# A short convolution's projections by Strassen's scheme, and a first stage with three modulators on TensorE

## The chip, the cores and the metric

The kernel runs on one core of one Trainium2 chip. The metric is the device time of one execution in microseconds, as the median of the runs shown. Engines are named TensorE (PE in the rows, PEld for its weight loads), VectorE (DVE), ScalarE (ACT), GpSimd (POOL) and SyncE (SP, which issues most DMAs).

## The reference

Two blocks work on 512 tokens of width 1024, all in fp32. The first is an adaptively normalised attention block. Its modulators are products of one vector `c` with a 1024 x 3072 matrix; the first third shifts and the second scales the normalised input:

```
mod = c @ w_ada[l] + b_ada[l]
shift, scale, gate = jnp.split(mod, 3, axis=-1)
h = rms_norm(x, g_pre[l]) * (1.0 + scale[:, None, :]) + shift[:, None, :]
proj = h @ w_in[l]
```

Attention of several kinds and two output projections follow. The second block puts 16 meta tokens ahead (528 tokens) and runs a gated short convolution and then an mLSTM mixer. The convolution, where most of the change lies, is

```
proj = u @ w_in                                   # (528 x 1024) @ (1024 x 8192)
b_gate, c_gate, xin, z = jnp.split(proj, 4, axis=-1)
y = conv_general_dilated(c_gate * xin, w_conv, ...)  # width 3, per channel
return (jax.nn.silu(z) * b_gate * y) @ w_out      # (528 x 2048) @ (2048 x 1024)
```

## The kernel before

Every fp32 operand of a large product is split in two fp32r parts, high and low, and each product is three matmuls (high by high, high by low, low by high; `mm3`). Activations lie with channels on the partitions: `uh` and `ul` hold the parts of the block's input as 8 slices of 128 channels by 528 tokens. A weight unit is a tile of 128 x 1024 that SP loads into a ring of three (`wst`); ScalarE writes its high part (`whi`), VectorE the low part (`wlo`), each a ring of three. The class `Weights` hands the units out in the order of a list.

The instructions are not issued in the order of the source. `Plan` notes each operation with its reads and writes, and at the end of each phase a list scheduler (`flush`) fills one queue per engine from modelled durations (`cost`) and priorities (the order of the source, plus `plan.prio`). On the chip each queue then runs in order and waits on semaphores.

First stage: the input `x1` comes in eight DMAs; ScalarE squares it, TensorE sums the columns and spreads the reciprocal root (`stat_cols`, `cols_bc`). For each of 8 slices k a megabyte of `w_ada` is loaded (`ada`, a ring of three), VectorE multiplies it by `c` and sums it (`ada_mac`, 9 instructions on 128 x 256), TensorE turns the sum into two columns (`modmm`), ScalarE makes the high part of h and a copy (`mkh`), VectorE the low part, and 18 matmuls of 512 columns take it in. GpSimd normalises slices 2 to 7 and makes the weights' low parts. Runs of matmuls of ones (`warm`) lie between.

Convolution: 16 steps f, each with four units (c, x, z, b) of 128 output channels. A unit's 528 tokens are two halves of 264 columns with a PSUM bank each: 2 halves x 8 slices x 3 = 48 matmuls. VectorE takes the banks out: c times `rb2`, times x, the three-tap convolution, z times `rb` and through tanh, b; GpSimd does two of the multiplications. After steps 4, 8, 12 and 15 `conv_out` projects four steps' results back (192 matmuls, four weight units) and adds them to `x1`.

## Time and profile before

| | us |
|---|---|
| median of 3 runs (lowest, highest) | 1488.86 (1488.4, 1491.43) |
| the profiled execution | 1492.32 |
| its span, first to last instruction | 1490.3 |
| TensorE busy in the span | 1453.2 |
| VectorE busy | 881.8 |
| ScalarE, GpSimd busy | 605.7, 251.5 |

The mean granted TensorE clock was 0.986 of full speed. A busy TensorE is not one at its peak: matmuls overlap, and the time from one start to the next is what counts. The same holds on VectorE, whose rows overlap by some 0.08 us.

### The profile page before, as it was taken

How to read it: one execution, taken by the hardware profiler on the slowest of the kernel's cores; microseconds unless marked ns; L12 is line 12 of the kernel's file. 1: busy time of each engine (PE TensorE's matmuls, PEld its weight loads, DVE VectorE, ACT ScalarE, POOL GpSimd, SP SyncE). 2: the span in 40 equal slices, each digit the busy share in tenths (PEclk: the TensorE clock that was granted, in tenths of full speed). 3: DMA queues.
4: the chain of work that ended last, by engine and by line, in shares of the span. 5: the costliest groups of instructions: out<-in, count | busy, mean ns of one | idle time of the engine just before them, and what ended most of it. 6: DMA issues, size and time to landing. Idle time of an engine off the chain costs nothing.

```text
span 1490.3 us, 22552 instructions
## 1 busy us (share of the span) xinstructions
PE 1453.2 (98%) x8965; PEld 1296.9 (87%) x8965; DVE 881.8 (59%) x1710; ACT 605.7 (41%) x1103; POOL 251.5 (17%) x296
## 2 busy tenths in 40 slices
PE   6899999999998999999999999999999999999997
PEld 5687888878898999999999999978878888887886
DVE  6976868786858745545445445755434635443465
ACT  3465747775256322122122122554333433433333
POOL 3220313342003111011010011302002001100201
PEclk7999999999998999999999999999999999999999
DMA  6535121013553222232222222321222222132221
GB/s 219 191 127 164 58 81 47 29 44 125 210 163 113 86 100 85 86 100 86 97 88 86 99 86 79 100 71 57 99 85 71 85 85 85 57 100 85 72 71 57
DMA packets 44120, 142.60 MB, mean 96 GB/s; under 512 B 5744, under 2 KB 12144, under 8 KB 42608
## 3 DMA queue, kind: packets, MB, share of 16 engines
q1 hardware_dynamic: 43440, 136.98, 27.7%
q0 software_dynamic: 576, 4.19, 0.8%
q8 instruction: 70, 1.15, 0.3%
q14 instruction: 34, 0.28, 0.1%
HBM read 139.06 MB, written 2.10 MB: 95 GB/s over the span
## 4 chain that ended last, share of the span: by engine, by line
PE 91%; DVE 6%; ACT 1%; DMA 1%; issue 0%; POOL 0%; SPq 0%; DVEq 0%; POOLq 0%; ACTq 0%
PE bank L255 91%; DVE mac L255 2%; DVE wlo L255 1%; DMA x<-in_xT 0%; DVE zt L255 0%; DVE ul L255 0%; DMA wst<-in_wm 0%; DVE P L255 0%; POOL P L255 0%; ACT whi L255 0%; ACT P L255 0%; DVE pl L255 0%; SPq L255 0%; DVE ak L255 0%; DVE so L255 0%
## 5 line engine op out<-in xcount | busy, mean ns | idle before, releaser
L255 PE MATMUL bank<-uh,whi 128*128 128x264 f32 (+1 forms) x1784 | 574.2, 326 | 3.2 <-ACT uh L255 2.1
L255 PE MATMUL bank<-ul,whi 128*128 128x264 f32 (+1 forms) x1784 | 572.2, 325 | 0.0
L255 PE MATMUL bank<-uh,wlo 128*128 128x264 f32 (+1 forms) x1768 | 568.4, 325 | 1.8 <-DVE wlo L255 1.8
L255 ACT CAST whi<-wst 128x1024 fp32r<-128x1024 f32 (+2 forms) x236 | 244.7, 1038 | 606.0 <-PE bank L255 445.6
L255 DVE TENSOR_TENSOR wlo<-wst,whi 128x1024 fp32r<-128x1024 f32 (+1 forms) x227 | 280.3, 1236 | 177.5 <-ACT whi L255 176.3
L255 PEld LDWEIGHTS bank<-uh,whi 128*128 128x128 f32 x1784 | 337.0, 189 | 28.9 <-ACT uh L255 3.7
L255 PEld LDWEIGHTS bank<-ul,whi 128*128 128x128 f32 x1784 | 336.7, 189 | 24.5 <-DVE ul L255 0.2
L255 PEld LDWEIGHTS bank<-uh,wlo 128*128 128x128 f32 x1768 | 334.3, 189 | 26.3 <-DVE wlo L255 2.2
L255 DVE TENSOR_TENSOR zr<-bank,rb 128x264 f32<-128x264 f32 (+1 forms) x64 | 35.8, 560 | 120.8 <-PE bank L255 120.8
L255 DVE TENSOR_TENSOR x<-x,bank 128x264 f32<-128x264 f32 (+2 forms) x102 | 49.8, 496 | 69.5 <-PE bank L255 67.4
L255 POOL TENSOR_TENSOR yv<-yv,rb 128x528 f32<-128x528 f32 x16 | 21.2, 1324 | 332.1 <-DVE yv L255 332.1
L255 PE MATMUL bank<-gh,wlo 128*128 128x264 f32 x256 | 72.5, 284 | 0.0
L255 PE MATMUL bank<-gl,whi 128*128 128x264 f32 x256 | 72.4, 283 | 0.0
L255 PE MATMUL bank<-gh,whi 128*128 128x264 f32 x256 | 72.3, 284 | 0.0
L255 POOL TENSOR_SCALAR P<-P,sm 128x256 f32<-128x256 f32 (+3 forms) x96 | 52.2, 562 | 81.9 <-DVE sm L255 41.4
L255 PE MATMUL bank<-whi,uh 128*128 128x512 f32 (+1 forms) x160 | 61.7, 386 | 0.3 <-DVE ak L255 0.3
L255 PE MATMUL bank<-wlo,uh 128*128 128x512 f32 (+1 forms) x160 | 61.7, 386 | 0.0
L255 PE MATMUL bank<-whi,ul 128*128 128x512 f32 (+1 forms) x160 | 61.6, 385 | 0.0
L255 ACT ACTIVATE P<-P,nm 128x256 f32<-128x256 f32 (+3 forms) x96 | 50.9, 531 | 9.8 <-DVE nm L255 8.6
L255 PE MATMUL bank<-Gh,whi 128*128 128x512 f32 (+1 forms) x144 | 53.5, 371 | 0.0
L255 PE MATMUL bank<-Gl,whi 128*128 128x512 f32 (+1 forms) x144 | 53.3, 370 | 0.0
L255 PE MATMUL bank<-Gh,wlo 128*128 128x512 f32 (+1 forms) x144 | 53.3, 370 | 0.0
(338 smaller groups left out, 2283.1 us busy)
## 6 DMA issues: line engine op xcount, KB each, us to landing
wst<-in_wci SPq DMA_DIRECT2D x64, 512.0 KB, 3.4
wst<-in_wqkv SPq DMA_DIRECT2D x32, 512.0 KB, 3.4
wst<-in_wzo SPq DMA_DIRECT2D x32, 512.0 KB, 3.4
wst<-in_wm SPq DMA_DIRECT2D x23, 512.0 KB, 3.5
wst<-in_wout SPq DMA_DIRECT2D x16, 512.0 KB, 4.0
wst<-in_wco SPq DMA_DIRECT2D x16, 512.0 KB, 3.4
wst<-in_wmo SPq DMA_DIRECT2D x16, 512.0 KB, 3.4
ada<-in_wada SPq DMA_DIRECT2D x7, 1024.0 KB, 5.0
```

Of the source, the lines that this page charges most:

```text
L255: call(*[v.real() if isinstance(v, View) else v for v in args], **{k: v.real() if isinstance(v, View) else v for k, v in kw.items()})
```

## The change

In the convolution, steps 0 and 1 stay as they were. From step 2 on, units are taken in pairs (c with x, z with b), and a pair's product is made by Strassen's scheme in Winograd's form: the 1024 input channels are two halves, the tokens are two halves, the two units are the third pair of halves, and seven products of 12 matmuls take the place of eight. `sums_of_u` makes four sums of the halves of u once (t1 to t4, each split in high and low; they lie in the memory of `QS`). For each pair four weight tiles are split: "a" (a unit as it is), "q" and "r" (sums of quarters), "d" (half a unit). The sums of "q" are made in memory: SP loads two half tiles, then two DMAs from GpSimd add another half to each (`accum_op`). `PairWeights` keeps how many tiles of each kind are out ("st" and "w" three, "q" two, "hq" and "hr" one). Between products ScalarE copies a bank while it is still being added to (`snap`), four times a pair.

One of the convolution's taps moves from VectorE to ScalarE; one multiplication by GpSimd moves to VectorE. In the first stage the input comes in four DMAs; slices 0, 1 and 4 get their modulator from eight fp32 matmuls with `c` as the stationary column (`mod_pe`); x is no longer normalised in place, VectorE multiplies by scale and `rbc` in one instruction; the low parts of weights are made by VectorE; two of three `warm` runs go. Some tiles are bound to memory early (`early=True`), and the planner's costs of matmuls and of GpSimd's DMAs change.

```
...
         if eng == "PE":
             fast = views[1].tile.dtype != F32
             if method == "transpose":
                 return 0.109, 0.1, None, 0
             m = _free(views[1])
             if fast:
-                return max(n / 2400.0 + 0.003, m / 1200.0), 0.1, None, 0
+                return max(n * 0.000445 + 0.005, m / 1200.0 + 0.002), 0.1, None, 0
             return 4 * max(n / 2400.0, min(m, 128) / 2400.0) + 0.003, 0.1, None, 0
         scalars = sum(isinstance(v, View) and _free(v) == 1 for v in list(args[2:]) + [kw.get("bias"), kw.get("scale")])
...
+class PairWeights:
...
+        self.cap, self.out = {"st": 3, "w": 3, "q": 2, "hq": 1, "hr": 1}, {}
+        self.loads, self.splits = [], []
+        self.at, self.st, self.parts = 0, {}, {}
+        for n, it in enumerate(items):
+            self.loads.append((n, "load", it))
+            if len(it) == 2:
+                self.loads += [(n, "sums", it), (n, "load_d", it)]
+            self.splits += [(n, x) for x in ("aqrd" if len(it) == 2 else "p")]
...
+    def load(self, n, what, it):
+        SP, G = self.plan.sp, self.plan.pool
+        if not self.take("q" if what == "sums" else "st"):
+            return False
+        if what == "sums":
+            t = self.tile("sq", 2)
+            SP.dma_start(t[:, :512], it[0][:, :512])
+            SP.dma_start(t[:, 512:], it[1][:, 512:])
+            for e in range(2):
+                G.dma_start(out=t[:, 512 * e:512 * e + 512], in_=it[1][:, :512], accum_op=OP.add)
+        else:
+            t = self.tile("wst", 3, pool=self.W.pool)
+            if what == "load":
+                SP.dma_start(t, it[0])
+            else:
...
+    def split(self, n, what):
+        V, A = self.plan.dve, self.plan.act
+        src = {"q": "sums", "r": "sums", "d": "load_d"}.get(what, "load")
+        if (n, src) not in self.st or not self.take({"q": "hq", "r": "hr"}.get(what, "w")):
+            return False
+        t = self.st[n, src]
...
+        else:
+            hi, lo = self.parts[n, what] = [self.tile(x + what, 1, F32R) for x in "hl"]
+            if what == "q":
+                A.copy(hi, t)
+                V.tensor_tensor(lo, t, hi.bitcast(F32), op=OP.subtract)
+            else:
+                q, st = self.st.pop((n, src)), self.st.pop((n, "load"))
+                t = self.pool.tile([128, 512], F32, name="sr", tag="sr", bufs=1)
+                for e in range(2):
+                    h = slice(512 * e, 512 * e + 512)
+                    V.tensor_tensor(t, t if e else q[:, 512:], st[:, h], op=OP.add)
+                    A.copy(hi[:, h], t)
+                    V.tensor_tensor(lo[:, h], t, hi[:, h].bitcast(F32), op=OP.subtract)
+                self.give("st")
+                self.give("q")
...
+    def done(self, what):
+        del self.parts[self.at, what]
+        self.give({"q": "hq", "r": "hr"}.get(what, "w"))
+        self.advance()
...
-    for f in range(16):
-        add("wci", range(4 * f, 4 * f + 4))
-        if f % 4 == 0 and f:
-            add("wco", range(f - 4, f))
-    add("wco", range(12, 16))
+    add("wci", 8)
+    n_first = len(units)
+    conv_items = []
+    for f in range(2, 16):
+        conv_items += [(a["wci"][4 * f], a["wci"][4 * f + 1]), (a["wci"][4 * f + 2], a["wci"][4 * f + 3])]
+        if f % 4 == 0:
+            conv_items += [(a["wco"][i],) for i in range(f - 4, f)]
...
+        def mod_pe(k):
+            t = adas.pop(k)
+            pr = bank((1, 256), (6, 7))
+            for q in range(KT):
+                PE.matmul(pr, vec[:, V_C + q:V_C + q + 1], t[:, q], start=(q == 0), stop=(q == KT - 1))
+            row = sp.tile([1, 256], F32, name="row", tag="row", bufs=2)
+            A.copy(row, pr)
+            pm = bank((128, 2), (6, 7))
+            for j in range(2):
+                PE.matmul(pm[:, j:j + 1], row[:, j * 128:j * 128 + 128], ones[0:1, 0:1], start=True, stop=True)
...
         def mkh(k):
             t = sp.tile([128, S], F32, name="ht", tag="ht", bufs=3)
...
-            A.activation(hh[:, k], x1[:, k, META:], AF.Identity, bias=Sc[:, k:k + 1], scale=Gc[:, k:k + 1])
-            A.activation(t, x1[:, k, META:], AF.Identity, bias=Sc[:, k:k + 1], scale=Gc[:, k:k + 1])
-            V.tensor_tensor(hl[:, k], t, hh[:, k].bitcast(F32), op=OP.subtract)
...
+            V.scalar_tensor_tensor(t, x1[:, k, META:], Gc[:, k:k + 1], rbc, op0=OP.mult, op1=OP.mult)
+            A.activation(hh[:, k], t, AF.Identity, bias=Sc[:, k:k + 1])
+            V.scalar_tensor_tensor(hl[:, k], t, Sc[:, k:k + 1], hh[:, k].bitcast(F32), op0=OP.add, op1=OP.subtract)
...
+        ON_PE = (0, 1, 4)
+        def mod(k):
+            if k in ON_PE:
+                mod_pe(k)
             else:
...
-                warm(14, rc0[:, 0:1].to_broadcast([128, 128]))
...
+            W.split_to(k + 2)
             if k + 2 < KT:
-                G.tensor_tensor(x1[:, k + 2, META:], x1[:, k + 2, META:], rbc, op=OP.mult)
-                m = ada_mac(k + 2)
-            W.split_to(k + 2, G if k + 1 < KT else None)
+                mod(k + 2)
+                mkh(k + 2)
...
-            t = sp.tile([128, KT, 256], F32, name="ada2", tag="ada2", bufs=1)
+            t = sp.tile([128, KT, 256], F32, name="ada2", tag="ada2", bufs=1, early=True)
...
+        half = {n: [[t[:, k:k + 2, b] for k in (k0, k0 + 2)] for t in (uh, ul)]
+                for n, k0, b in (("11", 0, B0), ("21", 4, B0), ("22", 4, B1))}
+        tv = [QF[:, n * T:(n + 1) * T] for n in range(15)] + [sp.tile([128, T], F32R, name="t4l")]
+        tv = [t.rearrange("p (k t) -> p k t", k=2) for t in tv]
+        half.update({f"t{j + 1}": [tv[4 * j:4 * j + 2], tv[4 * j + 2:4 * j + 4]] for j in range(4)})
...
+        def sums_of_u(kk):
...
+                A.activation(tmp[:, hs], x1[:, k, B1], AF.Copy, scale=w)
+                t1, t2, t3, t4 = (t[:, hs] for t in ts)
+                V.scalar_tensor_tensor(t1, x1[:, k, B0], w, tmp[:, hs], op0=OP.mult, op1=OP.subtract)
+                V.scalar_tensor_tensor(t2, x1[:, k + 4, B1], n4, t1, op0=OP.mult, op1=OP.subtract)
+                V.scalar_tensor_tensor(t3, x1[:, k + 4, B1], w4, tmp[:, hs], op0=OP.mult, op1=OP.subtract)
+                V.scalar_tensor_tensor(t4, x1[:, k + 4, B0], n4, t2, op0=OP.mult, op1=OP.subtract)
+            for j, t in enumerate(ts):
+                t = t.rearrange("p (k t) -> p k t", k=2)
+                h, l = (v[kk] for v in half[f"t{j + 1}"])
+                A.copy(h, t)
+                V.tensor_tensor(l, t, h.bitcast(F32), op=OP.subtract)
...
+        def product(ps, what, e, u, first):
+            w = SW.part(what)
+            for k in range(4):
+                c = slice(512 * e + 128 * k, 512 * e + 128 * k + 128)
+                mm3(ps, (w[0][:, c], w[1][:, c]), [v[k // 2][:, k % 2] for v in half[u]], first and k == 0, k == 3,
+                    not first)
...
+        def pair():
+            x, y, z = (bank((128, HALF)) for _ in range(3))
+            product(x, "a", 0, "11", True)
+            product(y, "q", 1, "t1", True)
+            p1 = snap(x)
+            product(x, "r", 0, "t2", False)
+            p5 = snap(y)
+            product(y, "r", 1, "22", False)
+            SW.done("r")
+            u2 = snap(x)
+            product(x, "q", 0, "t3", False)
+            SW.done("q")
+            product(z, "a", 1, "21", True)
+            SW.done("a")
+            u3 = snap(x)
+            product(x, "d", 0, "t4", False)
+            SW.done("d")
+            SW.at += 1
+            return x, y, z, p1, u2, u3, p5
...
+            A.activation(yv, cxt[:, 0:T], AF.Copy, scale=cw[:, 3 * f:3 * f + 1])
             for j in (1, 2):
                 V.scalar_tensor_tensor(yv, cxt[:, j:j + T], cw[:, 3 * f + j:3 * f + j + 1], yv, op0=OP.mult, op1=OP.add)
             G.tensor_tensor(yv, yv, rb, op=OP.mult)
...
+        def cx_tile():
+            t = sp.tile([128, T + 2], F32, name="cx", tag="cx", bufs=2)
+            V.memset(t[:, 0:2], 0.0)
+            return t
+        def gate_z(yv, zr):
+            tz = sp.tile([128, T], F32, name="tz", tag="tz", bufs=1)
+            A.activation(tz, zr, AF.Tanh, scale=0.5)
+            V.scalar_tensor_tensor(zr, tz, 1.0, zr, op0=OP.add, op1=OP.mult)
+            V.tensor_tensor(yv, yv, zr, op=OP.mult)
...
-            G.tensor_tensor(yv, yv, zr, op=OP.mult)
...
+        rms_half_bc(1, sp, tagged(sp, "zr", T))
+        bps = proj2(kview(W.get(0), KT), [bank((128, HALF), (6 + e,)) for e in range(2)])
+        gv0 = plain(0, *conv_ps, bps)
+        plan.prio = 30
+        sums_of_u(0)
+        sums_of_u(1)
...
+        for f in range(2, 16):
+            x, y, z, p1, u2, u3, p5 = pair()
+            cs = sp.tile([128, T], F32, name="cs", tag="cs", bufs=1)
+            cxt = cx_tile()
+            both(z, p1, y, u2, cs)
+            V.tensor_tensor(u3, u3, p5, op=OP.add)
+            V.tensor_tensor(cs, cs, rb2, op=OP.mult)
+            V.tensor_tensor(cxt[:, 2:2 + HALF], cs[:, B0], x, op=OP.mult)
+            V.tensor_tensor(cxt[:, 2 + HALF:], cs[:, B1], u3, op=OP.mult)
+            yv = conv(f, cxt)
+            x, y, z, p1, u2, u3, p5 = pair()
+            zr = sp.tile([128, T], F32, name="zr", tag="zr", bufs=2)
+            both(z, p1, y, u2, zr)
+            V.tensor_tensor(u3, u3, p5, op=OP.add)
+            V.tensor_tensor(zr, zr, rb, op=OP.mult)
+            gate_z(yv, zr)
+            gv = sp.tile([128, T], F32, name="gv", tag="gv", bufs=2)
+            V.tensor_tensor(gv[:, B0], yv[:, B0], x, op=OP.mult)
+            V.tensor_tensor(gv[:, B1], yv[:, B1], u3, op=OP.mult)
+            g_parts(f, gv)
             if f % 4 == 0:
...
```

## Rows read from the trace of the kernel before

**Rows 1.** The page's first part: busy time, share of the span, instructions.

```profile
PE 1453.2 (98%) x8965; PEld 1296.9 (87%) x8965; DVE 881.8 (59%) x1710; ACT 605.7 (41%) x1103; POOL 251.5 (17%) x296
```

**Rows 2.** The chain that ended last: start us, us, what.

```profile
26.23 9.96 DVE mac L255 x7
...
470.48 1005.89 PE bank L255 x6553
```

**Rows 3.** Busy time of each engine, clock and DMA by stretch.

```profile
core 0: us, PE busy (x) PEld busy (x) DVE busy (x) ACT busy (x) POOL busy (x), PEclk, DMA share, GB/s
...
515.00:935.00 420.00, 420.00 (x3453) 420.00 (x3452) 207.42 (x334) 95.45 (x109) 42.44 (x32) 1.00 0.27 90
...
460.00:465.00 5.00, 4.32 (x37) 4.11 (x35) 5.00 (x9) 4.04 (x10) 3.58 (x2) 1.00 0.51 156
465.00:470.00 5.00, 1.24 (x8) 0.92 (x8) 5.00 (x9) 3.66 (x11) 2.84 (x4) 0.94 0.45 160
470.00:475.00 5.00, 4.52 (x20) 4.52 (x21) 3.06 (x10) 0.00 (x0) 1.03 (x1) 0.50 0.34 105
475.00:480.00 5.00, 5.00 (x26) 4.71 (x25) 3.60 (x7) 2.90 (x9) 1.75 (x2) 0.54 0.00 0
```

**Rows 4.** Matmuls in order of time, in the convolution: start us, us.

```profile
540.45 0.28 PE L255 MATMUL bank<-uh,wlo 128*128 128x264 f32 x1
540.57 0.28 PE L255 MATMUL bank<-uh,whi 128*128 128x264 f32 x1
```

**Rows 5.** VectorE in order of time, in the convolution.

```profile
562.23 0.76 DVE L255 SCALAR_TENSOR_TENSOR yv<-cx,cw,yv 128x528 f32<-128x528 f32 x1
562.91 0.42 DVE L255 TENSOR_TENSOR zr<-bank,rb 128x264 f32<-128x264 f32 x1
563.28 0.06 DVE L255 MEMSET cx<- 128x2 f32 x1
...
595.49 1.23 DVE L255 TENSOR_TENSOR wlo<-wst,whi 128x1024 fp32r<-128x1024 f32 x1 [0.57 <-ACT whi L255]
596.64 0.70 DVE L255 TENSOR_TENSOR gl<-gv,gh 128x528 fp32r<-128x528 f32 x1
```

**Rows 6.** Groups by shape: busy us, mean ns of one.

```profile
L255 ACT CAST whi<-wst 128x1024 fp32r<-128x1024 f32 x223 | 233.9, 1050 | 603.0 <-PE bank L255 445.6 <-issue 153.8 <-DMA wst<-in_wm 2.0
...
L255 DVE TENSOR_TENSOR pl<-bank,ph 128x512 fp32r<-128x512 f32 x54 | 36.0, 686 | 3.1 <-ACT ph L255 2.8
```

**Rows 7.** VectorE and GpSimd at 455 to 459 us, in order of time.

```profile
455.90 0.48 DVE L255 SCALAR_TENSOR_TENSOR ul<-x,vec,uh 128x264 fp32r<-128x264 f32 x1
...
458.91 0.95 DVE L255 SCALAR_TENSOR_TENSOR ul<-x,vec,uh 128x264 fp32r<-128x264 f32 x1
...
457.92 1.64 POOL L255 TENSOR_TENSOR x<-x,zt 128x248 f32<-128x248 f32 x1 [3.70 <-DVE zt L255]
```

**Rows 8.** DMA issues: KB each, median us to landing.

```profile
wst<-in_wci SPq DMA_DIRECT2D x64, 512.0 KB, 3.4
...
ada<-in_wada POOLq DMA_DIRECT2D x4, 1024.0 KB, 6.2
```

**Rows 9.** The first stage in order of time.

```profile
1.13 6.20 PE L255 MATMUL bank<-ones 128*128 128x128 f32 x36 [1.13 <-DVE epsc L255]
...
11.52 0.72 ACT L255 ACTIVATE mac<-x 128x256 f32<-128x256 f32 x2 [0.39 <-DMA x<-in_xT]
...
12.64 6.33 PE L255 MATMUL bank<-rc,ones 128*128 128x128 f32 x28 [1.47 <-DVE rc L255]
...
14.37 0.34 DVE L255 TENSOR_SCALAR mac<-ada,vec 128x256 f32<-128x256 f32 x1
...
44.53 3.08 DVE L255 SCALAR_TENSOR_TENSOR mac<-ada,vec,mac 128x256 f32<-128x256 f32 x6
...
76.29 1.52 PE L255 MATMUL bank<-uh,wlo 128*128 128x512 f32 x6
...
77.65 1.52 PE L255 MATMUL bank<-ul,whi 128*128 128x512 f32 x6
```

More of the change, by code (lines that the diff above doesn't have):

```diff
@@ L164, in tile @@
         t = Tile(self, list(shape), dtype, name, f"{tag}_{k}", ring[1][k])
+        if early and ring[1][k] is None:
+            t.bind()
         ring[1][k] = t
@@ L638, in trunk @@
         sp = pool(sx, "sp")
-        acc = [bank(among=(i,)) for i in range(6)]
-        ss = sp.tile([128, S], F32, name="ss")
         rbc = sp.tile([128, S], F32, name="rbc")
@@ L711, in trunk @@
-        modmm(0, m)
-        warm(6, rbc[:, 256:384])
+            V.scalar_tensor_tensor(t, x1[:, k, META:], Gc[:, k:k + 1], rbc, op0=OP.mult, op1=OP.mult)
+            A.activation(hh[:, k], t, AF.Identity, bias=Sc[:, k:k + 1])
+            V.scalar_tensor_tensor(hl[:, k], t, Sc[:, k:k + 1], hh[:, k].bitcast(F32), op0=OP.add, op1=OP.subtract)
+        for k in range(3):
+            ada_load(k)
+            W.load_to(k + 1)
+        wb = bank((128, 128), (6,))
+        for _ in range(18):
+            PE.matmul(wb, ones, ones, start=True, stop=True)
@@ new lines, in trunk @@
+        ss = rbc
+        for k in range(KT):
+            sq = sp.tile([128, S], F32, name="sq", tag="ht", bufs=3) if k else ss
+            A.activation(sq, x1[:, k, META:], AF.Square)
+            if k:
+                V.tensor_tensor(ss, ss, sq, op=OP.add)
+        rc0 = sp.tile([128, 4], F32, name="rc0")
+        stat_cols(ss, 0, S, rc0, (6, 7))
+        cols_bc(rc0, S, sp.tile([128, S], F32, name="dg", tag="ht", bufs=3), rbc, (6, 7))
+        acc = [bank(among=(i,)) for i in range(6)]
+        ON_PE = (0, 1, 4)
@@ L1269, in ev_b @@
                 V.tensor_tensor(gv[:, HS[e]], yv[:, HS[e]], pb[e], op=OP.mult)
[L1270 to L1286 removed]
+            return gv
@@ new lines, in trunk @@
+        rms_half_bc(1, sp, tagged(sp, "zr", T))
[4 more added lines that the diff above has]
+        sums_of_u(1)
+        plan.prio = 0
+        g_parts(0, gv0)
+        ps = [proj2(kview(W.get(2 - q if q < 3 else 0), KT), [bank((128, HALF), (2 * q + e,)) for e in range(2)])
+              for q in range(4)]
+        SW.advance()
+        g_parts(1, plain(1, *ps))
```

200 lines of the change are left out of this document (116 added, 84 removed).

## The prediction

> **What bounds the kernel now.** I read the page first: TensorE is busy 1453.2 us of a span of 1490.3 [rows 1], so only fewer matmul cycles or fewer TensorE gaps can shorten it. The chain that ended last says where the gaps are [rows 2]. From 470.48 us on it is TensorE for 1005.89 us without a break; near its start stand nearly 10 us of one modulator sum on VectorE. The stretches confirm it [rows 3]: in the convolution, 515 to 935 us, TensorE is busy 420.00 of 420.00 us at full clock, VectorE 207.42 and ScalarE 95.45. There the price of a matmul is its distance to the next one, 0.12 us for 264 columns [rows 4]; its row's 0.28 us contains the overlap. So a matmul removed from this stretch is worth 0.12 us for as long as the other engines keep up, and the question is whether VectorE, half idle now, still does.
>
> **The matmuls removed.** Steps 2 to 15 have two pairs each, 28 in all. A pair was 2 units x 48 = 96 matmuls and becomes 7 x 12 = 84. 28 x 12 x 0.12 = 40.3 us less.
>
> **What VectorE gets for it.** I price by distance of starts [rows 5]: 1.15 for 128x1024 (595.49 to 596.64), 0.68 for the multiply-add of 528, 0.37 for 264 columns. Rows thus overlap by 0.08, so 528 columns (0.70) cost 0.62, and 512 columns, 0.686 in a row [rows 6], cost 0.61. Per pair the splits are: "a" and "q" 2 x 1.15; "r" two additions and two subtractions, 4 x 0.61; "d" 0.61; together 5.35, 10.7 per step (before: four units, 4.6). The evacuation of a step has ten instructions of 264 columns (3.7), four of 528 (2.5: two by `rb` or `rb2`, the gate's product that GpSimd had, the low part), the gate's multiply-add (0.63) and two taps (1.36): 8.2. Together 18.9 us per step against TensorE's 168 x 0.12 = 20.2: 94% full, where before it was half. After steps 4, 8, 12 and 15 `conv_out` gives TensorE 192 x 0.12 = 23 us and VectorE only 16 x 0.37 + 4 x 1.15 = 10.5, so a backlog is worked off there.
>
> ScalarE has, per pair, 1.05 for "a" and for "q" [rows 6], some 0.55 for each of three half tiles and 0.36 (my estimate from 264/1024 of that row plus its start) for each of four copies of a bank: 5.2, and per step three more of about 0.63: 12.3 of 20.2. It is hidden by TensorE; but a bank's copy must end within the next product of 12 matmuls, 1.45 us, and can stand behind one 1.05 us split. 1.05 + 0.36 is just inside. If that cover is gone, TensorE waits some tenths.
>
> GpSimd keeps one multiplication per step. While it adds, a VectorE instruction with two operands in SBUF takes 0.95 instead of 0.48 [rows 7], 0.47 more. One collision per step makes 19.4, still under 20.2. The Trainium skill ("SBUF — State Buffer", "Who interferes with whom") says that of two such instructions the second fully blocks until the first finishes. By that the collision costs up to the length of GpSimd's row, 1.64 here, and VectorE would need 20.5, a hair over TensorE; the trace shows both merely stretched, so I keep 0.47.
>
> I put the losses at two places. At the changeover, VectorE must fit both plain steps' evacuation (16), `sums_of_u` (16 multiply-adds of 264 at 0.40 and 8 subtractions of 528 at 0.62: 11.4) and the first splits (four or five plain ones and 5.35 for the first pair: 10.5) into about 35 us: it is full, and a miss of the first "q" or t1 stops TensorE. I take 5 us, from 0 to 12 (all of `sums_of_u` late). In the steps, with VectorE at 94 to 96%, an instruction often finds it taken; there is one "q" tile, rewritten between product 5 of one pair and product 2 of the next (4 x 1.45 - 1.45 = 4.3 us, for 1.05 + 1.15 and their queue). I take a third of a microsecond per pair, 9 us; bounds 0 and 22 (0.8 per pair, about two thirds of one split's length).
>
> **The transfers.** Per pair SP issues 1.25 MB and GpSimd 0.5 MB, against 1 MB before, in 10.1 us: 173 GB/s beside 90 [rows 3], at 0.27 of the engines; hidden. SP's queue is in order: a half tile that waits for its sum slot holds "d" and the next unit behind it. GpSimd's `yv` multiplication stands behind its additions, which wait for SP's landings; its result is wanted only a pair later, so it is covered. The trace has no adding DMA. Nearest rows [rows 8]: 3.4 us to land for 512 KB from SP, 6.2 for 1 MB from GpSimd. I bound it by 3.4 and 12.4 (6.2 once to read and once to write) and take 6.2, being GpSimd's own. A sum slot then lives 3.4 + 6.2 + 1.05 + 1.15 + 0.61 = 12.4 us and two slots turn in two pairs, 20.2: nothing is paid up to a landing of 14 us.
>
> **The first stage.** Its last matmuls end at 77.65 + 1.52 = 79.2 us [rows 9]. The input has landed at 11.52. Then came 28 passes of ones, 6.33 us, now gone, and VectorE work slowed by GpSimd: seven sums in 9.96 us [rows 2] where six take 3.08 undisturbed [rows 9]. After: two squares, a sum, column sums and spreading, about 5 us, so `rbc` at 16.5. The first modulator is on TensorE, its matrix there by 14.4 (VectorE's first use). An fp32 pass of 128 columns is 0.17 (6.20/36) or 0.23 (6.33/28) [rows 9]; eight matmuls of 256 columns, at two passes each and once or twice the pass, are between 2.7 and 7.3 us; I take 5, as the clock is low there. With row copy, columns, scaling and high part the first useful matmul stands at 22.5. From there VectorE leads: a slice with its sum costs 3.1 + 0.9 for the sum, 0.45 for columns, 2 x 0.61 plus scalars (1.4), a weight's low part 0.86: 6.7, less overlap 6.2; one without 2.7. 5 x 6.2 + 3 x 2.7 = 39, begun at about 20: 59, and 18 matmuls (0.227 each, 76.29 to 77.65) behind it: 63 to 64. That is 15 us less. Bounds: TensorE with 7.3 per modulator at a low clock ends at 74 (5 less); at 2.7 it ends at 59 (20 less).
>
> The other edits (early binding, planner costs, layout of the input) are 0 with 3 either way: the rest of the span is TensorE-bound already [rows 2].
>
> **Sum.** 40.3 + 15 - 5 - 9 = 41.3 less. The profiled execution took 1492.32, 2.0 more than its span and 3.5 more than the median. 1492.3 - 41.3 = 1451.0 there, so 1447.5 for the median.
>
> **Rivals.**
> VectorE becomes the bound. If its instructions come at their rows' length (32 a step, 0.08 each) it needs 19.4 + 2.6 = 22, and every step is 1.8 longer than TensorE's share. For: no stretch before had it so full with such chains. Against: it ran back to back at the shorter distance [rows 5]. 14 x 1.8 = 25 in place of 9: 1463.5. If the changeover costs 12 as well, 1470.
>
> The adding DMAs are late. From a landing of 14 us each further one costs half of it per pair; at 17, 28 x 1.5 = 42 eats all: slower than before from there on, 1517 at 20 less the 9 no longer paid, about 1500. Against: 17 is nearly three times GpSimd's 1 MB.
>
> The clock falls: this one ends slower. When TensorE was busy only 1.24 of 5 us, the granted clock was 0.50 and 0.54 for the next ten, 1.2 in place of 2.4 GHz; with 4.32 of 5 it stayed at 1.00 [rows 3]. Short waits for a bank's copy or "q" in every product could hold it at the lower level in part of the 28 x 84 x 0.12 = 282 us. Each tenth of them costs 28 us; from 15% on the kernel is slower, at 30% 1532. Against: the waits I expect are far shorter than those before 470 us. The Trainium skill ("TensorE: Matmul & The Clock Gate", "A second HAM failure mode: psum-queue depth-cycling") describes this very case, short idles between groups that cycle banks; no stretch of this trace shows it.
>
> No stall at all: the planner's order holds on the chip, and the first stage gives 20: 1447.5 - 14 - 5 = 1428.5.
>
> **Chances and range.** My forecast 0.72, VectorE the bound 0.13, no stall 0.06, adding DMAs 0.05, clock 0.04. Bounds of the forecast: 1428.5, and 1447.5 + 10 + 7 + 13 = 1477.5. Range 1428 to 1480, leaving out the last two and some of the tails. What a measurement of this kernel can tell from no change is about 0.2%, 3 us. Faster 0.9 (all but the last two cases, and part of the adding DMAs), same 0.02, slower 0.08.
>
> **What would show it.** After the change I expect 336 matmuls less; the first stage's last matmul near 64 us; TensorE busy all but about 14 us of the convolution, idle mostly within 10 us of the first pair; VectorE at some 90% from there to the last step; the clock at 1.00 but for a dip at the changeover; adding DMAs landing in 4 to 12 us with nobody waiting for them. A clock under 1.00 in the steps, a "q" split that waits for a DMA, or long waits for ScalarE's bank copies would each prove the forecast wrong.

## The result, and the profile after

The changed kernel takes 1449.1 us (1448.9 to 1449.9), against 1489.7 for the kernel before in the same comparison (1488.4 to 1491.4): a ratio of 0.973, 95% interval 0.971 to 0.975. That is 40.6 us less; 41.3 were forecast and the predicted time was 1447.5. The profiled execution has a span of 1447.4 us, against 1490.3 before, 42.9 less. (The profiled execution of the kernel before was 2.6 us over this median, so spans make every gain a little larger than medians do.)

The page's first part, to be held against [rows 1]:

```profile
PE 1416.5 (98%) x8629; PEld 1247.8 (86%) x8629; DVE 995.8 (69%) x1910; ACT 703.5 (49%) x1312; POOL 259.6 (18%) x322
```

There are 8965 - 8629 = 336 matmuls less, as the change says; VectorE has 114 us more, ScalarE 98 us more. Busy time by stretch, columns as in [rows 3], first the way into the convolution and then its steps:

```profile
451.00:456.00 5.00, 1.52 (x11) 1.10 (x9) 5.00 (x10) 3.16 (x7) 2.32 (x2) 1.00 0.50 150
456.00:461.00 5.00, 3.88 (x19) 3.84 (x19) 4.24 (x11) 1.23 (x5) 2.73 (x2) 0.58 0.68 215
461.00:466.00 5.00, 5.00 (x32) 4.83 (x32) 1.33 (x4) 0.72 (x4) 0.35 (x1) 0.73 0.41 152
...
500.00:505.00 5.00, 5.00 (x43) 5.00 (x42) 5.00 (x10) 1.63 (x2) 0.00 (x0) 1.00 0.18 56
505.00:510.00 5.00, 2.82 (x23) 2.61 (x22) 5.00 (x9) 2.38 (x5) 0.00 (x0) 1.00 0.00 2
...
541.00:562.00 21.00, 20.65 (x170) 20.44 (x169) 19.91 (x32) 12.15 (x22) 4.90 (x6) 1.00 0.72 169
562.00:583.00 21.00, 21.00 (x173) 20.87 (x172) 18.98 (x33) 10.98 (x18) 4.88 (x5) 1.00 0.79 202
583.00:605.00 22.00, 22.00 (x183) 22.00 (x183) 13.98 (x26) 6.21 (x9) 1.78 (x2) 1.00 0.43 112
```

The reader is to see three things. The stretch from 451 us has the same hole and the same dip of the clock as the stretch from 465 us had in [rows 3]: it is no work of the change. VectorE is busy 5.00 of 5 us at the changeover and 19.91 of 21 in a step, 95%, yet TensorE has 20.65 of 21 there and all of it in the next two rows. The third of these, 583 to 605 us, is output products: VectorE has 14 of 22 to do and works off what it owes. The clock is 1.00 in all of them.

TensorE's waits from 480 to 905 us (engine and tile, what was waited for: us in total, times, longest):

```profile
PE bank L260 <- DVE wlo L260: 2.2, 1, 2.2
PE bank L260 <- ACT sn L260: 1.0, 4, 0.4
PE bank L260 <- DVE ul L260: 0.5, 1, 0.5
```

One wait of 2.2 us for a low part at the changeover, and four of at most 0.4 us for the copy of a bank: nobody on TensorE waits for a transfer. The adding DMAs are the second of these lines of the page's last part:

```profile
sq<-in_wci SPq DMA_DIRECT2D x56, 256.0 KB, 3.4
sq<-in_wci POOLq DMA_DIRECT2D x56, 256.0 KB, 5.3
```

Where the 42.9 us came from is read from moments that both traces have: the first copy out of the first stage's banks, the first product of the `Th` tiles, the last product of the `gh` tiles, and the end.

| stretch | before | after | difference | forecast |
| --- | --- | --- | --- | --- |
| start to first copy (`ak`) | 78.08 | 66.11 | -12.0 | -15 |
| to first `Th` product | 340.09 | 340.00 | -0.1 | 0 |
| to last `gh` product | 526.50 | 492.76 | -33.7 | -26.3 |
| to the end | 545.6 | 548.5 | +2.9 | 0 |

Two terms are off by 3 us against the kernel, one by 7 in its favour. A stretch of a single profile is good to about 2 us: two kernels of the experiments below, with the same instructions in the same order up to there, have their first copy at 66.05 and 64.38 us. For the third row I also summed what the distances of TensorE's starts exceed 0.12 us per matmul: from the last `Th` product to the end of the first Strassen step (451.7 to 545) it is 13.9, and 10.0 in the corresponding 464 to 557 us before: 3.9 lost at the changeover. From 541 to 899 us it is 3.8 (0.5 of it ahead of 545), before 0. The forecast had 5 and 9.

The first stage, TensorE in order of time, to be read beside [rows 9]:

```profile
13.75 1.86 PE L260 MATMUL bank<-ada,vec 128*1 128x256 f32 x4 [0.35 <-ACT rc L260]
15.54 2.08 PE L260 MATMUL bank<-ht,ones 128*128 128x128 f32 x8
17.55 3.91 PE L260 MATMUL bank<-ada,vec 128*1 128x256 f32 x12
21.91 0.60 PE L260 MATMUL bank<-ones,row 1*128 1x1 f32 x4 [0.45 <-ACT row L260]
22.44 3.61 PE L260 MATMUL bank<-ada,vec 128*1 128x256 f32 x16
25.99 1.43 PE L260 MATMUL bank<-uh,whi 128*128 128x512 f32 x5
...
65.68 1.52 PE L260 MATMUL bank<-ul,whi 128*128 128x512 f32 x6
```

The same stage by stretches:

```profile
16.00:22.00 6.00, 5.55 (x21) 2.55 (x20) 0.00 (x0) 1.09 (x3) 0.00 (x0) 0.67 0.72 289
...
26.00:36.00 10.00, 10.00 (x47) 7.73 (x47) 9.73 (x25) 2.79 (x5) 0.00 (x0) 1.00 0.74 280
36.00:46.00 10.00, 10.00 (x47) 6.36 (x46) 9.39 (x23) 3.33 (x5) 0.00 (x0) 1.00 0.78 288
```

The first modulator's 16 fp32 passes take 1.86 + 3.91 = 5.8 us around the spreading (5 were taken). But the first useful matmul stands at 25.99 and not at 22.5: between the first slice's columns (21.91) and it are the second modulator's 16 passes. VectorE does nothing at all from 16 to 22 us. From 26 us on TensorE is busy 10.00 of 10, so what is late at 26 stays late to the last matmul, which ends at 67.2.

### The profile page after: what moved, and what is told of

It reads as the page before. It is cut to its first block, busy times and chain, and to the rows that moved or that the text cites. A ratio compares the mean times of both kernels' runs of the same rounds, so it can differ in the third digit from the quotient of the medians.

```text
span 1447.4 us, 22545 instructions
## 1 busy us (share of the span) xinstructions
PE 1416.5 (98%) x8629; PEld 1247.8 (86%) x8629; DVE 995.8 (69%) x1910; ACT 703.5 (49%) x1312; POOL 259.6 (18%) x322
## 4 chain that ended last, share of the span: by engine, by line
PE 84%; DVE 9%; ACT 2%; issue 2%; POOL 1%; DMA 1%; SPq 0%; DVEq 0%; ACTq 0%; POOLq 0%
PE bank L260 84%; DVE wlo L260 2%; DVE ul L260 1%; DVE zr L260 1%; DVE zt L260 1%; POOL P L260 1%; DVE x L260 1%; DVE num L260 0%; DVE yv L260 0%; ACT whi L260 0%; DMA x<-in_xT 0%; ACT hq L260 0%; DMA wst<-in_wm 0%; DVE qs L260 0%; DVE so L260 0%
## 5 line engine op out<-in xcount | busy, mean ns | idle before, releaser
L260 ACT CAST whi<-wst 128x1024 fp32r<-128x1024 f32 (+3 forms) x236 | 232.5, 987 | 353.4 <-PE bank L260 300.3
L260 PE MATMUL bank<-uh,whi 128*128 128x512 f32 (+1 forms) x1112 | 380.0, 348 | 2.8 <-ACT whi L260 1.9
L260 DVE TENSOR_TENSOR wlo<-wst,whi 128x1024 fp32r<-128x1024 f32 (+3 forms) x235 | 269.9, 1151 | 161.7 <-ACT whi L260 160.4
L260 PE MATMUL bank<-ul,whi 128*128 128x512 f32 (+2 forms) x1112 | 379.5, 348 | 1.6 <-DVE ul L260 1.6
L260 PE MATMUL bank<-uh,wlo 128*128 128x512 f32 (+1 forms) x1096 | 375.3, 349 | 4.8 <-DVE wlo L260 4.8
L260 PEld LDWEIGHTS bank<-uh,whi 128*128 128x128 f32 x1112 | 209.4, 189 | 28.5 <-ACT whi L260 2.1
L260 PEld LDWEIGHTS bank<-uh,wlo 128*128 128x128 f32 x1096 | 206.9, 189 | 29.6 <-DVE wlo L260 5.5
L260 PEld LDWEIGHTS bank<-ul,whi 128*128 128x128 f32 (+1 forms) x1112 | 209.0, 188 | 26.2 <-DVE ul L260 2.3
L260 PE MATMUL bank<-qs,hq 128*128 128x264 f32 x448 | 84.5, 285 | 0.0
L260 PE MATMUL bank<-qs,whi 128*128 128x264 f32 (+1 forms) x296 | 77.2, 334 | 1.0 <-ACT sn L260 1.0
```

The costliest lines, as they stand in the source:

```text
L260: call(*[v.real() if isinstance(v, View) else v for v in args], **{k: v.real() if isinstance(v, View) else v for k, v in kw.items()})
```

## The experiments

Three questions: which part gave what; how near VectorE and the adding DMAs are to being the bound, as the rivals have it; and why the last stage, which the change hardly touches, became longer. All kernels were timed against the kernel before on the same chip (its median was between 1488.9 and 1490.3), so a difference between kernels of two comparisons can be off by up to 1 us. An edit of the program also makes the planner find another order, and the third run below shows 6.7 us from the order alone: a difference of a few microseconds can have that cause as well as the one that the edit is meant to test.

**The first stage as it was.** The changed kernel with the old first stage:

```diff
-    for k in range(0, KT, 2):
-        SP.dma_start(x1[:, k:k + 2, META:], a["xT"][:, k:k + 2])
+    for h in range(0, S, 256):
+        for k in range(0, KT, 2):
+            SP.dma_start(x1[:, k:k + 2, META + h:META + h + 256], a["xT"][h // 256, :, k:k + 2])
...
-        mod(0)
-        W.split_to(1)
...
+        modmm(0, m)
+        warm(6, rbc[:, 256:384])
         mkh(0)
...
```

> The changed kernel with the first stage, the input's layout and its loading as they were. Theory: the first stage gave 12.0 us and nothing behind it depends on how it is done, so this kernel is 12 us slower than the changed one, about 1461 (29 below the kernel before), and the convolution keeps its gaps. Rival: the stage's gain shifted the transfers and the order of the work behind it as well; then the difference from the changed kernel is not 12, but 8 or less, or 16 and more. The prediction had 15.

Measured: 1464.4 us (ratio 0.983, 0.982 to 0.985), 15.3 over the changed kernel; by what each gained over the kernel before in its own comparison (24.5 and 40.6) it is 16.1. That is the rival's size and not the theory's. Its first copy stands at 79.66 us, 13.6 later than in the changed kernel and 1.6 later than in the kernel before, where the stage is the same but the order of its instructions is another. The convolution is 2.9 us longer than in the changed kernel. This pointed to something that touches the order everywhere.

**The first stage alone.** The kernel before with the same lines the other way round, all else untouched.

> The kernel before with only the new first stage and the new layout of the input. Theory: 12 us faster than before, about 1477.5, and the last stage as before (none of the 2.9 us that the changed kernel loses there). Together with the kernel that keeps the old first stage the two parts add up to the whole change, 40.6. Rival: part of the gain is taken up again by a later wait; then less than 9.

Measured: 1478.5 us, 10.4 less than before (ratio 0.993, 0.992 to 0.994; so 8.6 to 12.4). Its first copy is at 65.50 us, 12.6 earlier than in the profiled execution of before, which was itself longer than the median; from the last `gh` product to the end it takes 546.1, as before. The two parts give 10.4 + 24.5 = 34.9, not 40.6: they don't simply add up, so the theory's last sentence failed.

**The planner's old price of a matmul.** The changed kernel with

```diff
-                return max(n * 0.000445 + 0.005, m / 1200.0 + 0.002), 0.1, None, 0
+                return max(n / 2400.0 + 0.003, m / 1200.0), 0.1, None, 0
```

> The changed kernel with the planner's old price of a matmul (0.113 us for 264 columns in place of 0.1225), and so another order of the same instructions. Theory: the 2.9 us that the last stage became longer come from the order that the new price gives; with the old price they come back, 1446, while the convolution may lose 1 to 3. Rival: the last stage's loss has nothing to do with the price; then the last stage is as long as in the changed kernel, and the time is the same or slightly worse for the order in the convolution.

Measured: 1442.4 us (ratio 0.969, 0.967 to 0.970), 6.7 less than the changed kernel, and the same instructions. The convolution did not lose. Its waits of TensorE from 480 to 905 us are this one line, and a step and the changeover look so:

```profile
PE bank L260 <- DVE wlo L260: 3.5, 2, 2.5
```

```profile
500.00:505.00 5.00, 3.92 (x33) 3.89 (x33) 5.00 (x10) 1.00 (x3) 0.00 (x0) 1.00 0.16 54
505.00:510.00 5.00, 2.54 (x21) 2.33 (x20) 5.00 (x8) 2.08 (x4) 0.00 (x0) 1.00 0.01 2
510.00:515.00 5.00, 5.00 (x31) 5.00 (x30) 5.00 (x12) 0.62 (x1) 0.00 (x0) 0.66 0.75 261
...
541.00:562.00 21.00, 21.00 (x175) 21.00 (x174) 20.36 (x33) 12.28 (x22) 6.44 (x6) 1.00 0.76 183
```

In the steps TensorE has lost all its waits: the excess over 0.12 per matmul is 0.5 us in 350, with VectorE at 20.36 of 21. At the changeover it is worse off (15.9 in place of 13.9, and the clock fell to 0.66 behind it). By spans, 1447.4 to 1442.8, the old price gives 1.7 in the middle of the kernel, 1.2 net in the convolution and 1.7 in the last stage. Over all profiles of this document the last stage takes 545.7 to 546.8 us with the old price and 546.9 to 549.1 with the new one. So most of the last stage's 2.9 is the price, and the rest is no more than profiles differ by.

**A price lower still**: `max(n / 2640.0 + 0.003, m / 1200.0)` in the same line.

> The changed kernel with the planner's price of a matmul lower still (0.103 us for 264 columns; old 0.113, new 0.1225, measured 0.12). Theory: a low price makes the planner hold TensorE to be ahead, so that it puts weights and sums earlier and the measured steps have no gaps: as with the old price within 2 us (1440.5 to 1444.5). Rival: the order is a matter of chance; then it is anywhere from 1440 to 1452, nearer to the changed kernel's 1449 than to 1442.

Measured: 1442.9 us (0.968, 0.967 to 0.970). Two low prices give the same total; the price nearest to the measured distance of 0.12 gives the worse order. For the steps this is as the theory has it, since TensorE has no gap in them with either low price:

```profile
541.00:891.00 350.00, 350.00 (x2867) 349.85 (x2867) 296.21 (x491) 177.02 (x294) 75.28 (x63) 1.00 0.58 152
```

But the gain doesn't lie in the same stretches:

| stretch, us by the profile | new price | old price | lower still |
| --- | --- | --- | --- |
| start to first `Th` product | 406.1 | 404.4 | 401.8 |
| to last `gh` product | 492.8 | 491.6 | 492.9 |
| to the end | 548.5 | 546.8 | 548.1 |

With the lowest price the convolution as a whole gains nothing (its changeover loses what the steps gain), the last stage stays long, and the gain stands ahead of the convolution. So it is shown that the order matters by some 6 us and that two orders without gaps in the steps exist; the theory that a low price brings weights and sums in time everywhere is not shown, and that the two totals agree is in part chance. How the planner's choices follow from the price I did not trace.

**The second modulator on VectorE.** `ON_PE = (0, 4)` in place of `(0, 1, 4)` in the changed kernel.

> The changed kernel with the second modulator (k = 1) on VectorE, not on TensorE. Theory: in the changed kernel the first useful matmul stood at 26.0 us and not at 22.5 because 16 fp32 passes of the second modulator are ahead of it in TensorE's queue, while VectorE is idle for 6.8 us before it; on VectorE the sum of 3.1 us fits into that idle time, the first useful matmul comes at about 22.5, and the stage ends 2 to 3.5 us earlier: about 1446. Rival: from there on VectorE sets the stage's pace, as the prediction had it (6.2 us for a slice with its sum), and the second slice comes later by about as much; then the time stays within 1 us.

Measured: 1447.2 us (0.972, 0.970 to 0.973), 1.9 less, which the intervals don't separate from the changed kernel. The trace shows the two halves of it:

```profile
23.90 2.45 PE L260 MATMUL bank<-uh,whi 128*128 128x512 f32 x6 [1.99 <-ACT uh L260]
```

```profile
22.00:26.00 4.00, 2.10 (x6) 1.73 (x7) 4.00 (x10) 1.45 (x2) 0.00 (x0) 0.81 0.87 330
26.00:36.00 10.00, 10.00 (x45) 7.58 (x45) 9.14 (x23) 3.12 (x4) 0.00 (x0) 0.90 0.67 257
```

The first useful matmul comes 2.1 us earlier, at 23.90, but behind a hole of 2 us, and the clock is 0.81 and 0.90 where it was 1.00 with the passes ahead of it. The first copy is 0.9 us earlier (65.17), less than two profiles can differ by. While the passes stand in the way, TensorE has no hole and the clock is up; without them the lower clock takes part of the gain back. How much, these rows alone don't say.

**Both**, the old price and the modulator on VectorE:

> The changed kernel with the planner's old price of a matmul and the second modulator on VectorE. The old price alone gave 6.7 us (1442.4), the modulator alone 1.9 (1447.2), both against 1449.1. Theory: they act in different stretches and add up to 1440.5. Rival: the old price already put the first stage's matmuls in an order that needs no help; then 1442.4, the same as the old price alone.

Measured: 1444.9 us (0.970, 0.968 to 0.971): they don't add up. The intervals of this one and of the old price alone overlap, so whether it is worse is not settled; a gain is not seen.

**More work for VectorE.** In the changed kernel, behind the low part of each `q`, into the ring of the tile that the `r` sums use:

```diff
                 V.tensor_tensor(lo, t, hi.bitcast(F32), op=OP.subtract)
+                j = self.pool.tile([128, 512], F32, name="sr", tag="sr", bufs=1)
+                for _ in range(2):
+                    V.tensor_tensor(j, t[:, :512], hi[:, :512].bitcast(F32), op=OP.subtract)
```

> The changed kernel with two more VectorE subtractions of 512 columns per pair (of the q sums, into a tile that nobody reads), 2 x 0.61 us, so 2.4 more per step. The output is not touched. Theory: VectorE, busy 19.9 of 21 us in a step of the changed kernel, is within 1.2 us of being the bound of a step; then it needs 21.3 of TensorE's 20.2, and only the output products after every fourth step give some of that back: 8 to 17 us longer, with waits of TensorE for low parts or banks in the third and fourth step of each group. Rival: there is more slack than the prediction's sum says (busy time overlaps with waits that cost nothing): at most 3 us.

Measured: 1481.1 us, 32 over the changed kernel, far more than either theory. TensorE's first wait from 480 to 905 us, and a step:

```profile
PE bank L260 <- ACT hr L260: 16.6, 20, 1.3
```

```profile
654.00:676.00 22.00, 19.70 (x151) 18.66 (x150) 20.36 (x35) 11.08 (x20) 3.43 (x5) 1.00 0.62 156
```

VectorE is not full (20.36 of 22), and what TensorE waits for is the high part of `r`, which comes out of the very tile that the added instructions occupy. So this run tested a chain through one tile, not VectorE's time. It was made again with a tile of its own:

```diff
-                j = self.pool.tile([128, 512], F32, name="sr", tag="sr", bufs=1)
+                j = self.pool.tile([128, 512], F32, name="junk", tag="junk", bufs=1)
```

> Again the changed kernel with two further VectorE subtractions of 512 columns per pair, but written to a tile of their own and not to the one that the r sums use. The output is not touched. The first form cost 32 us (1481.1), nearly all of 28 x 1.22 = 34, yet VectorE was busy only 20.0 of 22 us there and TensorE waited for the high parts of r, which come out of that shared tile. Theory: VectorE's time alone is the price, each step being within 0.3 us of VectorE's bound already: 28 to 34 longer again. Rival: the shared tile's chain was most of it; with its own tile the cost is only what exceeds TensorE's 20.2 us in a step, less what the output products give back: 8 to 17 longer, 1457 to 1466.

Measured: 1453.7 us (0.976, 0.974 to 0.977): 4.6 over the changed kernel, for 28 x 1.22 = 34 us of further VectorE work. Less than both theories. Two steps and the output products behind them, and TensorE's longest wait in the steps:

```profile
541.00:562.00 21.00, 21.00 (x173) 20.88 (x172) 20.96 (x36) 12.19 (x21) 6.83 (x6) 1.00 0.68 171
562.00:583.00 21.00, 20.69 (x170) 20.48 (x169) 20.19 (x34) 10.79 (x18) 6.78 (x6) 1.00 0.77 209
583.00:605.00 22.00, 21.62 (x177) 21.41 (x177) 17.67 (x34) 6.40 (x9) 1.79 (x2) 1.00 0.45 120
```

```profile
PE bank L260 <- ACT sn L260: 2.3, 8, 0.3
```

VectorE is now full in a step (20.96 of 21, and 20.19 in the next), and in the output products it has 17.67 of 22 where the changed kernel had 13.98: the work that doesn't fit in the steps slides there. By these rows it is that room which keeps VectorE from being the bound; a run without output products in between was not made.

**The gate's product back on GpSimd**, `G.tensor_tensor(yv, yv, zr, op=OP.mult)` in `gate_z`:

> The changed kernel with one edit of the change undone: the gate's product yv * zr on GpSimd as before. Theory: VectorE saves 0.6 us of a step, but TensorE loses only some tenths to it in a step as it is, and GpSimd's 1.6 us rows stretch VectorE's by 0.5: the same within 2 us. Rival: steps of the changed kernel are held up by VectorE; then this is 3 to 6 us faster. Second rival: the product sits on the way from z to the gated value, is 1 us longer there and stands in GpSimd's queue behind adding DMAs that wait for a transfer; then 5 us or more slower.

Measured: 1453.6 us (0.976, 0.974 to 0.977), 4.5 slower. VectorE has 16 instructions less but is busy 999.0 us, not less than the 995.8 of the changed kernel: its rows beside GpSimd's take back what it saved. How, is read from a step of the changed kernel, with an undisturbed product of GpSimd as the last row:

```profile
554.27 0.69 DVE L260 TENSOR_TENSOR lr<-sr,hr 128x512 fp32r<-128x512 f32 x1
554.44 1.72 POOL L260 TENSOR_TENSOR yv<-yv,rb 128x528 f32<-128x528 f32 x1 [2.12 <-DVE yv L260]
554.99 1.71 DVE L260 TENSOR_TENSOR sr<-sr,wst 128x512 f32<-128x512 f32 x1
...
575.02 1.32 POOL L260 TENSOR_TENSOR yv<-yv,rb 128x528 f32<-128x528 f32 x1 [1.53 <-DVE yv L260]
```

GpSimd's product starts while `lr` runs and takes 1.72 in place of 1.32. VectorE's `sr` starts while the product runs, takes 1.71 in place of the 0.69 of a row of 512 columns, and ends 0.54 after the product: it stood until that was done, which costs VectorE 1.0 us. It is the same in the kernel before around the rows of [rows 7]:

```profile
453.41 0.82 POOL L255 TENSOR_TENSOR x<-x,zt 128x248 f32<-128x248 f32 x1 [61.75 <-DVE zt L255]
...
457.77 1.21 DVE L255 TENSOR_TENSOR wlo<-wst,whi 128x1024 fp32r<-128x1024 f32 x1
```

GpSimd's 1.64 us from 457.92 contain a wait for this `wlo`, as the same instruction takes 0.82 undisturbed, and VectorE's 0.95 us from 458.91 end 0.30 after GpSimd's row. The waits of TensorE from 480 to 905 us in the run with the gate's product on GpSimd:

```profile
PE bank L260 <- DVE wlo L260: 3.0, 1, 3.0
PE bank L260 <- DVE lq L260: 2.7, 5, 0.8
```

By moments the convolution is 5.4 us longer than in the changed kernel, 2.6 of it up to the first product of `hq`, the rest behind it, with waits for the low part of `q`; the last stage is 1.6 shorter, though the edit doesn't touch it. The loss is between what my theory and the second rival had; VectorE's slowdown, not GpSimd's queue, is where the waits point. That the other order has a part in the 4.5 us is not excluded.

**Each addition three times.** The adding DMAs in a loop of three, each waiting for the one before:

```diff
-            for e in range(2):
-                G.dma_start(out=t[:, 512 * e:512 * e + 512], in_=it[1][:, :512], accum_op=OP.add)
+            for _ in range(3):
+                for e in range(2):
+                    G.dma_start(out=t[:, 512 * e:512 * e + 512], in_=it[1][:, :512], accum_op=OP.add)
```

> The changed kernel with every adding DMA made three times in a row (each waits for the one before), so that a sum of weights is complete some 16 us after the first addition's issue instead of 5; the sums then hold the second unit three times, so the output is not the reference's. The prediction's rule: nothing is paid up to a landing of 14 us, and half of the excess per pair beyond it; 16 us would cost 28 x 1 = 28, so 1470 to 1485, with waits of VectorE and TensorE for the sums, and GpSimd's six issues of 0.9 us per pair alone fill 5.4 of 10.1 us. Rival: the transfers are so far ahead that the loop hides 16 us as well: within 3 us. A rival to both: the DMA queues are nearly full (share 0.73 to 0.79 in a step) and the further 1 MB per pair makes every weight late: over 60 us longer.

Measured: 1535.9 us, 87 over the changed kernel and slower than before (1.032, 1.029 to 1.034). A step of it:

```profile
562.00:583.00 21.00, 13.91 (x86) 12.54 (x84) 11.05 (x18) 6.72 (x12) 6.98 (x9) 0.84 0.78 155
583.00:605.00 22.00, 19.36 (x147) 18.31 (x148) 16.68 (x27) 9.24 (x14) 8.45 (x10) 1.00 0.93 209
```

The size fits the rival of full DMA engines, so that was taken as the theory for the next run. **The same with hardly any bytes**: two further additions of 32 columns in a row behind each of 512.

```diff
                 G.dma_start(out=t[:, 512 * e:512 * e + 512], in_=it[1][:, :512], accum_op=OP.add)
+            for _ in range(2):
+                for e in range(2):
+                    G.dma_start(out=t[:, 512 * e:512 * e + 32], in_=it[1][:, :32], accum_op=OP.add)
```

> The changed kernel with two further adding DMAs of 32 columns in a row behind each one of 512, so that a sum is complete later by two more landings and issues, with hardly more bytes; the sums then hold 32 columns of each half of the second unit three times, so the output is not the reference's. Three full ones cost 87 us, with the DMA engines busy 0.79 to 0.95 of a step. Theory: that was the DMA engines' time, not the delay; with 10 to 12 us until a sum is complete (under the prediction's 14) the time is the same as the changed kernel's within 3 us. Rival: the delay itself or GpSimd's issues (six of 0.9 us per pair) cost; then 30 us or more longer.

Measured: 1488.4 us, 39 over the changed kernel: the theory fell. The DMA engines are less busy in its steps (0.67) than in those of the changed kernel (0.72 and 0.79), and GpSimd's queue waits for landings. Its waits from 515 to 900 us, then two steps and a stretch with output products:

```profile
POOL sq L260 <- DMA sq<-in_wci: 132.8, 63, 11.7
```

```profile
542.00:564.00 22.00, 18.70 (x135) 16.83 (x134) 16.82 (x29) 11.02 (x18) 12.38 (x12) 1.00 0.67 142
564.00:586.00 22.00, 20.55 (x159) 19.72 (x160) 16.27 (x27) 7.93 (x15) 10.40 (x11) 1.00 0.67 162
...
610.00:632.00 22.00, 22.00 (x183) 22.00 (x182) 17.39 (x28) 12.23 (x21) 6.95 (x8) 1.00 0.55 130
```

GpSimd waits 63 times for a landing before it may issue the next addition (8 times in the changed kernel). A full addition lands 5.1 us after its issue in this run, a narrow one 3.5, an issue takes 0.9: the first narrow one goes out at 5.1, the third round at 5.1 + 3.5 = 8.6, its second half at 9.5. By these rows a sum would be complete after 13.0 us, and GpSimd would have 11.0 us of a pair's 10.1 to do with half of a multiplication of 1.3, so 28 x 0.9 = 25 of the 39 measured (my estimate). The trace has more: from the first issue of a pair to its last landing it is 16.2 us in the median (12.6 to 22.9), and over 14 in 23 of 28 pairs. By the prediction's rule, half of what exceeds 14 us per pair, this costs 28 x 1.1 = 31 us. So what fell is the delay that I had expected, and not the rule. Nor is GpSimd's queue full by itself, for in the steps it waits for VectorE too:

```profile
568.84 3.58 POOL L260 DMA_DIRECT2D sq<-in_wci  x4 [5.76 <-DVE lr L260]
```

Whether the queue or the two slots for sums set the pace is not shown; each holds up the other here, and part of the 16.2 us may be the delay itself. Of the 87 us some 39 are thus had with hardly any bytes; that the rest is the DMA engines' time was not shown separately.

**The sums of the activations later.** The kernel with the old price, and

```diff
-        plan.prio = 30
+        plan.prio = 90
```

> The kernel with the planner's old price (1442.4), and the sums of the activations put back by 90 places of its order in place of 30. Theory: the loss at the changeover, some 4 us of TensorE there (2.6 and 1.2 waiting for the low parts of two plain weights), is one of order: VectorE makes the second half of the sums before weights that are wanted earlier. With those weights first, 2 to 3.5 us less, 1439 to 1440.5. Rival: VectorE has no idle time there at all, so that what is put back is late for the first Strassen products instead, and TensorE waits as long there: the same within 1 us.

Measured: 1442.9 us (0.968, 0.967 to 0.970), the same as with 30. The changeover:

```profile
PE bank L260 <- DVE wlo L260: 5.8, 2, 4.0
```

```profile
500.00:505.00 5.00, 3.30 (x28) 3.09 (x26) 5.00 (x12) 3.03 (x6) 0.00 (x0) 1.00 0.00 0
505.00:510.00 5.00, 2.70 (x14) 2.70 (x15) 5.00 (x7) 0.08 (x1) 0.00 (x0) 0.79 0.31 97
```

VectorE is full in either order (5.00 of 5). (The line of waits is of 449 to 545 us, where the kernel with 30 has 5.4 for `wlo`.) Putting the sums back only makes another thing late. In both orders that were tried the loss stays, which fits a loss by VectorE's amount of work, as it was forecast, and not by its order.

## Why the prediction was right, and where it was not

The forecast of the time held because its main terms did, and because three terms that were mis-sized nearly cancelled: the first stage 3.0 too good, the last stage 2.9 too good, the convolution's losses 7.4 too bad. That the time came out within 1.6 us is luck.

- **The matmuls removed** (40.3): 336 less, at a distance of 0.12 as taken. Right.
- **VectorE at 94% of a step**: 19.91 of 21 us, 95%, and 90% in the next. Right (from 545 to 883 us, output products included, it is 85%, where "some 90%" was expected), and so is ScalarE's 12.3 of 20.2 (12.15 of 21). That VectorE leaves TensorE alone is shown by the run with 34 us more of its work, which costs 4.6. The rival with VectorE as the bound (25 us) needed the rows' full length to count; it didn't. A chain through one tile is what comes first: when the single `sr` tile was held 1.2 us longer per pair, 32 us were lost, where the same work in a tile of its own cost 4.6.
- **The changeover** (5): 3.9. **The steps** (9, a third of a us per pair): 3.8 in the changed kernel and 0.5 with the old price. The term was right in kind (the 0.4 us waits are for a bank's copy, as worked out) but too large, and it was no price of the scheme: an order exists in which it is nearly zero. That order comes nearest to the rival without stalls; its 1428.5 was out of reach by the changeover, 5.9 there, and by the first stage.
- **GpSimd's collisions**: here a reading failed. 0.47 per collision was kept against the Trainium skill's rule ("SBUF — State Buffer", "Who interferes with whom"), by which the second instruction waits for the whole first. The trace agrees with the rule: in the steps VectorE's row ends only after GpSimd's and takes 1.0 us more (a row of `lq` at 661.74 us even 2.37 in place of 1.22), and [rows 7] show the same and no mere stretch. The price for `yv`'s product is thus 1.0, and a step needs 19.9 of 20.2 us in place of 19.4. That still fits, so the time doesn't hang on it; the 20.5 that the prediction worked out took a GpSimd row that held a wait of its own.
- **The adding DMAs**: 5.3 us to land where 6.2 were taken, and nobody waits. "Nothing is paid up to a landing of 14 us" is not refuted: the run with narrow additions, with 16.2 us for a sum, lost 39 where the rule gives 31. What it left out is that additions which wait for each other stand in one queue on GpSimd, so that a chain takes longer than its landings add up to. The DMA engines, too, are busier than the bytes suggest: 0.72 to 0.79 in a step, where before had 0.27. The rival of late additions was added up wrongly: at 20 us its own rule gives 28 x 3 = 84, less 9, so 1522.5 and neither 1517 nor 1500.
- **The first stage** (15): 12.0 by the profile, 10.4 (8.6 to 12.4) by itself. The step that failed is "the first useful matmul stands at 22.5": the second modulator's passes, 3.6 us, are ahead of it on TensorE, and I had counted only the first one's. With the second modulator on VectorE it stands at 23.90, so 1.4 of the 3.5 us are not these passes. The last matmul ends at 67.2 where "near 64" was expected. "From there VectorE leads" was wrong too: TensorE is busy 10.00 of 10 us from 26 us on.
- **The other edits** (0, 3 either way): the planner's new price, counted there, costs 6.7 us by medians and 5.9 by the gains over before, 4.6 of it by spans. This is the one term outside its bounds, and part of two of the three differences above hangs on it, the last stage's and the convolution's. Early binding and the planner's cost of GpSimd's DMAs were not timed alone.
- **The clock**: 1.00 in every step, as forecast; none of the 0.2 to 0.4 us waits lowered it. The Trainium skill's warning ("TensorE: Matmul & The Clock Gate", "A second HAM failure mode: psum-queue depth-cycling") is thus not seen here with waits as short as these. The dip that I expected at the changeover did not come in the changed kernel, but it did with the old price. The sign "idle mostly within 10 us of the first pair" did not follow from the sum, which had 9 of 14 us in the steps.

The steps with their measured sizes, by medians: 1488.9 before, 1478.5 with the new first stage, 1442.4 with Strassen's scheme and the old price, 1449.1 with the new price. The version with the old price beats both kernels: 46.5 us less than before, 6.7 less than the change.

## What to carry to other kernels

An engine at 95% of a loop did little harm here, where a stretch that needs less of it comes round every few steps; what bit earlier was a chain through a tile with a single buffer, and a chain of transfers in one queue of which each waits for the one before. A long row beside another engine's can be a wait: see whether it ends just after the other. Where a planner orders the instructions, its prices are part of every change: time them alone, for the price nearest to the measurement gave the worse order here, and look at the stretches, for two equal times came from different ones. And a matmul that is added for one slice stands in TensorE's queue ahead of the first useful one of another; count all of them.

## What the runs showed of the hardware

An adding DMA of 256 KB lands 5.3 us after its issue, against 3.4 for a plain one of the same size in the same stage, and each issue holds GpSimd about 0.9 us; one of 16 KB takes 3.5 all the same. VectorE's additions and subtractions of two operands in SBUF stand while GpSimd multiplies there, and the other way round: 0.69 us became 1.71 beside a product of 1.32 us, which became 1.72. An fp32 pass of 256 columns over one column of weights costs 0.226 us at full clock (3.61 for 16) and 0.465 (1.86 for 4) from 13.75 us, where the granted clock was 0.50. Holes of a like size had different consequences: with TensorE busy 2.82 of 5 us between stretches of 5.00, the clock stayed at 1.00; with 3.92 and then 2.54, it fell to 0.66 in the next five.
